# The 256-token level of a gated linear attention, taken through the state at token 256

## The chip, the cores and the metric

The kernel runs on one core of a Trainium2 chip. A core has TensorE (PE, matrix multiplication, results in PSUM), VectorE (DVE), ScalarE (ACT), GpSimd (POOL) and SyncE (SP, which here issues DMAs). The metric is the device time of one execution in microseconds (us), as the median of several runs.

## The reference

One decoder layer over 512 tokens of width 1024: a layer norm, then gated linear attention (GLA) and latent attention side by side, then an MLP. The change lies in the GLA, four heads with keys of 128 and values of 256:

```python
def step(state, inp):
    qi, ki, vi, gi = inp
    b = jnp.cumsum(gi, axis=2)
    b_last = b[:, :, -1:, :]
    diff = b[:, :, :, None, :] - b[:, :, None, :, :]
    decay = jnp.exp(jnp.where(causal[:, :, None], diff, -jnp.inf))
    scores = jnp.einsum('bhid,bhjd,bhijd->bhij', qi, ki, decay)
    o = jnp.einsum('bhij,bhjv->bhiv', scores, vi) + jnp.einsum('bhid,bhdv->bhiv', qi * jnp.exp(b), state)
    state = jnp.exp(b_last)[:, :, 0, :, None] * state + jnp.einsum('bhjd,bhjv->bhdv', ki * jnp.exp(b_last - b), vi)
    return state, o
```

In short, token i receives for each earlier token j the value v_j with the weight sum over d of q_id k_jd times the decay of channel d from j to i.

## The kernel before

Activations lie with features on the 128 partitions and the 512 tokens along the free dimension, in blocks of 128 tokens. Nearly every product is taken in three matmuls: each fp32 operand is split into a high part (a copy rounded to the format fp32r, on ACT) and a low part (the remainder, on DVE), by the helper `split` (lines 109 to 115), and high x high, high x low and low x high are summed in PSUM.

**Levels.** The kernel doesn't use chunks of 64 but a tree over the tokens. For s = 1, 2, 4 ... 256, level s covers the pairs (j in the left half, i in the right half) of each stretch of 2s tokens. `gla_levels(h)` (line 790) keeps one tile `qk` a head, [128, 2, 512]: plane 0 holds keys, plane 1 queries. `update(s)` multiplies left keys and right queries by their decays, so that before level s the keys carry the decay to the end of their half and the queries the decay from its start; a level is then a plain product of keys and queries. Levels up to 64 are put with masks into the four diagonal 128x128 blocks `SD`, later split to `sd`; level 128 makes the two blocks `s128`; level 256 makes the four blocks of scores between tokens 0 to 255 and tokens 256 to 511 in plain fp32 (lines 872 and 873: for each key block, 128 keys against 256 queries), and `take` splits them into `s256` (lines 829 and 830).

**Output.** `gla_out(h)` (line 896) sums the output of query block i over the key blocks j <= i: scores (weights) times values `vh`, `vl` (moving, 256 columns), three matmuls a block pair, ten block pairs a head. Two query blocks share a PSUM bank (`ps`). Then come the mean square (line 920), the gate, and transposes into `ogT` (line 936), which `y_gla` reads after the gates' projections and `mla_qr(0)`.

**What sets the order.** The levels and the outputs are two lanes of generators (`lane_levels`, `lane_out`, one head after the other) that are stepped from inside the projections' matmul loops, `gemm_tm` (lines 281 to 283), `proj_r` (752 to 754) and the gates' `unit` (1210 to 1212). The order so traced gives priorities; the order on each engine is then fixed at build by a scheduler that follows a simulated timeline (line 1681). PSUM tiles come from two pools of four banks, `MM` for projections and `PX` for nearly all of the GLA. Weights are loaded into three `wraw` buffers and split on ACT and DVE at lines 191 and 192, ahead of their use.

Of the kernel before, what the change touches and what calls it, by code (L numbers as in the profile page):

```python
# [52 lines left out]
def tile_hybrid_block(ctx: ExitStack, tc: tile.TileContext, I, out, dbg=None):  # L53
# [19 lines left out]
    def A(shape, dt=F32, n="a"):  # L73
        tag, bufs = ("C", 8) if n in TAG_C else (n, TAG_W[n]) if n in TAG_W else ("A", 24)
        return pa.tile(shape, dt, tag=tag, bufs=bufs, name=nm(n))
# [14 lines left out]
    def PX(shape=(P, T), dt=F32, n="px"):  # L90
        return px.tile(list(shape), dt, tag="px", name=nm(n))
# [17 lines left out]
    def split(src, hi, lo, scale=None):  # L109
        if scale is None:  # L110
            act(hi, src, AF.Copy)
            return vtt(lo, src, f(hi), op=ALU.subtract)
        else:
            act(hi, src, AF.Copy, scale=scale)
            return stt(lo, src, scale, f(hi), op0=ALU.mult, op1=ALU.subtract)
# [674 lines left out]
    def gla_levels(h):  # L790
        qk = QK[h]
        QK[h] = None
        if h == 0:
            decays(0)
        D, DS[h] = DS[h], None
        k0 = qk[:, 0, :]
        off = {s: 2 * T - 2 * T // s for s in (1, 2, 4, 8, 16, 32, 64, 128)}
        SD = B([P, NT, P], F32, "SD")
        s128 = s256 = None

        def update(s):
            v = lr(qk, s)
            vtt(v, v, view(D, off[s] + 1, (2, T // (2 * s)), (-1, 2), (0, s)), op=ALU.mult)

        def pack(s):
            M = B([P, T], F32, "M")
            if s == 128:
                act(M.rearrange("p (n two s) -> p n two s", two=2, s=s), lr(qk, s), AF.Copy)
            else:
                for i, w in enumerate((T + 256 + s, T + s - 256)):  # L810
                    act(pairs(M[:, i * 256:(i + 1) * 256], s), view(k0, i * 256, (2 * s, 128 // s), (w, 2), (1, s)), AF.Copy)
            return M

        def put(dst, src, s, w):
            mk = (lmask, lmask2)[1 - w][:, LEVELS.index(s), :].rearrange("p (n s) -> p n s", s=s)
            nc.vector.copy_predicated(dst.rearrange("p t (n two s) -> p t n two s", two=2, s=s)[:, :, :, w, :],
                                      mk[:, None].to_broadcast([P, 2, 64 // s, s]), src)

        def take(s, p):
            nonlocal s128, s256  # L820
            if s <= 64:
                v = p[:, :256].rearrange("p (t n two s) -> p t n two s", t=2, two=2, s=s)
                for i, w in enumerate((1, 0)):
                    put(SD[:, 2 * i:2 * i + 2], v[:, :, :, w, :], s, w)
            elif s == 128:
                s128 = B([P, 2, 2, P], F32R, "s128")
                split(p[:, :256].rearrange("p (a b) -> p a b", b=P), s128[:, 0], s128[:, 1])
            else:
                s256 = A([P, 2, 2, 2 * P], F32R, "s256")
                split(p.rearrange("p (a b) -> p a b", b=256), s256[:, 0], s256[:, 1])  # L830

        x0 = B([P, T], F32, "x0")
        act(x0.rearrange("p (a c) -> p a c", a=2), view(k0, 0, (T + 256, 2), (1, 256)), AF.Copy)
        xs = [B([P, 2, 192], F32, "x1") for _ in range(2)]
        for i, x in enumerate(xs):
            c = 2 * i * P
            act(x[:, :, :P], qk[:, 1 - i, c:c + 256].rearrange("p (t i) -> p t i", i=P), AF.Copy)
            vtt(x[:, :, P:], view(qk[:, 1 - i, :], c + 1 - i, (P, 2), (2, 64)), view(D, c + 1, (P, 2), (2, 64)), op=ALU.mult)
        v = view(k0, 0, (2, T // 2), (T, 2))
        vtt(v, v, view(D, 1, (2, T // 2), (-1, 2)), op=ALU.mult)  # L840
        v = view(k0, T + 1, (2, T // 2))
        vtt(v, v, D[:, T:T + T // 2], op=ALU.mult)
        Ms = [pack(2)]
        yield
        px1 = []
        for i in range(2):
            p = PX()
            for t in range(2):
                c = (2 * i + t) * P
                mm(p[:, t * 192:(t + 1) * 192], x0[:, c:c + P], xs[i][:, t, :], start=True, stop=True)  # L850
            px1.append(p)
        update(2)
        Ms.append(pack(4))
        yield
        for i, p in enumerate(px1):
            pt = p[:, :384].rearrange("p (t c) -> p t c", c=192)
            d = SD[:, 2 * i:2 * i + 2, :]
            vtt(d, pt[:, :, :P], ident[:, None, :].to_broadcast([P, 2, P]), op=ALU.mult)
            put(d, pt[:, :, P:].rearrange("p t (n s) -> p t n s", s=1), 1, 1 - i)
        prev, s = None, 2  # L860
        while s < T:
            p = PX()
            M = Ms.pop(0) if s < 256 else None
            if s <= 64:
                for i in range(2):
                    mm(p[:, i * P:(i + 1) * P], M[:, i * P:(i + 1) * P], M[:, 256 + i * P:256 + (i + 1) * P], start=True, stop=True)
            elif s == 128:
                for i in range(2):
                    mm(p[:, i * P:(i + 1) * P], M[:, 2 * i * P:(2 * i + 1) * P],
                       M[:, (2 * i + 1) * P:(2 * i + 2) * P], start=True, stop=True)  # L870
            else:
                for j in range(2):
                    mm(p[:, j * 256:(j + 1) * 256], qk[:, 0, j * P:(j + 1) * P], qk[:, 1, 256:], start=True, stop=True)
            if s <= 64:
                update(2 * s)
            if s <= 32:
                Ms.append(pack(4 * s))
            if prev is not None:
                take(*prev)
            prev = (s, p)  # L880
            s *= 2
            if s == 16 and h + 1 < GH:
                decays(h + 1)
            yield
        sd = A([P, 2, NT, P], F32R, "sd")
        act(sd[:, 0, :2], SD[:, :2], AF.Copy)
        gtt(sd[:, 1, :2], SD[:, :2], f(sd[:, 0, :2]), op=ALU.subtract)
        take(*prev)
        p = PX()
        for i in range(2):  # L890
            nc.tensor.transpose(p[:, i * P:(i + 1) * P], SD[:, 2 + i, :], ident)
        yield
        split(p[:, :256].rearrange("p (t i) -> p t i", i=P), sd[:, 0, 2:], sd[:, 1, 2:])
        SS[h] = (sd, s128, s256)

    def gla_out(h):
        while SS[h] is None or Vh[h] is None or rgn[h] < NT:
            yield
        sd, s128, s256 = SS[h]

        def blk(j, i, w):
            if i == j:
                return sd[:, w, i, :]
            if j // 2 == i // 2:
                return s128[:, w, j // 2, :]
            return s256[:, w, j, (i - 2) * P:(i - 1) * P]

        vh, vl = Vh[h]
        ss = S([P, NT], F32, "gss")
        ps = []  # L910
        for i in range(NT):
            if i % 2 == 0:
                ps.append(PX())
            o = ps[i // 2][:, (i % 2) * HV:(i % 2 + 1) * HV]
            for j in range(i + 1):
                mm(o, blk(j, i, 0), vh[:, j, :], start=j == 0, stop=False)
                mm(o, blk(j, i, 0), vl[:, j, :], start=False, stop=False)
                mm(o, blk(j, i, 1), vh[:, j, :], start=False, stop=j == i)
            sq = B([P, HV], F32, "osq")
            act(sq, o, AF.Square, accum_out=ss[:, i:i + 1])  # L920
            if i >= 1:
                yield
        vts(ss, ss, 4.0 / HV, 4.0 * RMS_EPS, op0=ALU.mult, op1=ALU.add)
        rs = S([P, NT], F32, "grs")
        gtt(rs, ss, mhalf[:, :NT], op=ALU.pow)
        yield
        og = [B([P, 2, HV], F32, "og") for _ in range(2)]
        for i in range(NT):
            o = ps[i // 2][:, (i % 2) * HV:(i % 2 + 1) * HV]
            stt(og[i // 2][:, i % 2, :], o, rs[:, i:i + 1], Rg[h][:, i, :], op0=ALU.mult, op1=ALU.mult)  # L930
        yield
        for kk in range(2):
            k = 2 * h + kk
            p = PX()
            for tt in range(NT):
                nc.tensor.transpose(p[:, tt * P:(tt + 1) * P], og[tt // 2][:, tt % 2, kk * P:(kk + 1) * P], ident)
            yield
            o = A([P, 2, T], F32R, "ogT")
            split(p, o[:, 0, :], o[:, 1, :], scale=glg[:, k:k + 1])
            ogT[k] = o  # L940
# [744 lines left out]
```

## Time and profile before

| | |
|---|---|
| median of 3 runs | 876.1 us (875.27 to 876.38) |
| the profiled execution | 876.66 us, of which the span 874.4 us |
| granted TensorE clock | 0.998 |
| TensorE busy | 857.4 us (98%) |
| DVE busy | 633.8 us (72%) |
| ACT busy | 469.4 us (54%) |
| line 873, matmuls of level 256 | 16 records, 120.5 to 206.2 us |
| lines 916 to 918, output blocks | 40 records each, 172.9 to 242.8 us |

A time in the trace counts from the start of the span. In a timeline's rows come start, duration, engine, line, operation, output and inputs by the program's names, shape and count; in brackets idle time of the engine before it and what ended it. Names lose their numbers, so `s` stands for `s128` and `s256`, and `px` for any tile of that pool. A matmul with fp32 operands appears as two records. Durations of matmuls overlap, so what one adds is read from the distance of the starts, or from the chain of waits, which counts each stretch of time once. Rows of waits give engine, tile and line, what was waited for, the total in us, the times and the longest.

### The profile page before, as it was taken

Reading aid. Unit: us, or ns where it says so; the run is one execution under the profiler, and the core shown is the slowest. Engines: PE = TensorE matmul, PEld = TensorE weight load, DVE = VectorE, ACT = ScalarE, POOL = GpSimd, SP = SyncE. Lnnn points to the kernel's source line nnn. Section 1 sums busy time; section 2 is a strip of 40 time slices with the busy share of each in tenths; the row PEclk is TensorE's granted clock in tenths of the full one; section 3 lists DMA queues with packets and bytes.
Section 4 is the critical chain, followed back from the end, with each engine's and each line's share of the span. In section 5 each row is a group of like instructions: output and inputs, shape, how many; then the busy total and the mean of one; then the engine's idle time right before and its main releaser. Section 6 shows DMA issues by size and latency. Waiting matters only on the chain.

```text
span 874.4 us, 12828 instructions
## 1 busy us (share of the span) xinstructions
PE 857.4 (98%) x4765; PEld 748.0 (86%) x4765; DVE 633.8 (72%) x1037; ACT 469.4 (54%) x821; POOL 143.8 (16%) x184
## 2 busy tenths in 40 slices
PE   6999999999999999999999999999999999999996
PEld 5988888889999988888888889988888888889985
DVE  7859989968566547567667878986567546788865
ACT  6546767746565625346545324575366446666820
POOL 0323304210110030300000022005301520141000
PEclk9999999999999999999999999999999999999999
DMA  7994946696646444323126446008922990498311
GB/s 248 273 240 143 335 149 157 202 276 209 145 146 151 135 112 126 80 55 103 49 85 256 142 143 219 1 1 243 262 73 49 296 212 22 101 240 223 118 62 76
DMA packets 95213, 134.57 MB, mean 154 GB/s; under 512 B 12672, under 2 KB 58112, under 8 KB 95152
## 3 DMA queue, kind: packets, MB, share of 16 engines
q1 hardware_dynamic: 73840, 92.36, 33.3%
q0 software_dynamic: 19392, 37.76, 19.9%
q10 hardware_dynamic: 1920, 3.66, 1.1%
q8 instruction: 37, 0.61, 0.3%
q14 instruction: 24, 0.20, 0.1%
HBM read 110.15 MB, written 8.91 MB: 136 GB/s over the span
## 4 chain that ended last, share of the span: by engine, by line
PE 91%; DVE 4%; DMA 3%; issue 1%; ACT 1%; SPq 0%; POOLq 0%; DVEq 0%; POOL 0%; ACTq 0%
PE mm L247 11%; PE mm L248 11%; PE mm L249 11%; PE mm L283 5%; PE mm L281 5%; PE mm L282 5%; PE mm L1212 4%; PE mm L1210 4%; PE mm L1211 4%; PE px L1496 2%; PE px L1497 2%; PE px L1498 2%; PE mm L754 1%; PE mm L753 1%; PE mm L752 1%; DMA res<-ev 1%
## 5 line engine op out<-in xcount | busy, mean ns | idle before, releaser
L192 DVE TENSOR_TENSOR wlo<-wraw,whi 128x1024 fp32r<-128x1024 f32 (+1 forms) x90 | 98.7, 1098 | 92.5 <-ACT whi L191 86.0
L191 ACT ACTIVATE whi<-wraw 128x1024 fp32r<-128x1024 f32 (+1 forms) x90 | 85.4, 949 | 92.2 <-PE mm L248 43.2
L248 PE MATMUL mm<-h,whi 128*128 128x512 f32 x224 | 87.2, 389 | 0.0
L247 PE MATMUL mm<-h,whi 128*128 128x512 f32 x224 | 87.1, 390 | 0.0
L249 PE MATMUL mm<-h,wlo 128*128 128x512 f32 x224 | 83.2, 390 | 0.0
L192 DVE TENSOR_TENSOR wlo<-wq,whi 128x1024 fp32r<-128x1024 f32 x44 | 54.0, 1227 | 28.9 <-ACT whi L191 28.8
L1515 POOL DMA_DIRECT2D res<-ev x42 | 37.5, 1030 | 184.8 <-ACT ev L1513 153.8
L191 ACT ACTIVATE whi<-wq 128x1024 fp32r<-128x1024 f32 x44 | 46.5, 1056 | 27.8 <-PE mm L1211 15.9
L1212 PE MATMUL mm<-sh,wlo 128*128 128x256 f32 x176 | 50.0, 284 | 0.0
L1211 PE MATMUL mm<-sh,whi 128*128 128x256 f32 x176 | 49.8, 283 | 0.0
L1210 PE MATMUL mm<-sh,whi 128*128 128x256 f32 x176 | 49.8, 283 | 0.0
L249 PEld LDWEIGHTS mm<-h,wlo 128*128 128x128 f32 x224 | 42.0, 188 | 9.1 <-DVE wlo L192 0.4
L248 PEld LDWEIGHTS mm<-h,whi 128*128 128x128 f32 x224 | 42.1, 188 | 8.7
L247 PEld LDWEIGHTS mm<-h,whi 128*128 128x128 f32 x224 | 42.0, 188 | 8.6
L191 ACT ACTIVATE xh<-wraw 128x1024 fp32r<-128x1024 f32 (+1 forms) x28 | 27.4, 986 | 28.2 <-PE mm L283 15.7
L192 DVE TENSOR_TENSOR xl<-wraw,xh 128x1024 fp32r<-128x1024 f32 (+1 forms) x28 | 31.3, 1128 | 8.7 <-ACT xh L191 8.7
L1558 ACT ACTIVATE relu<-mm 128x512 f32<-128x512 f32 x24 | 14.1, 595 | 41.9 <-PE mm L249 41.9
L1210 PEld LDWEIGHTS mm<-sh,whi 128*128 128x128 f32 x176 | 33.8, 192 | 0.0
L1211 PEld LDWEIGHTS mm<-sh,whi 128*128 128x128 f32 x176 | 33.8, 192 | 0.0
L1212 PEld LDWEIGHTS mm<-sh,wlo 128*128 128x128 f32 x176 | 33.8, 192 | 0.0
L1212 PE MATMUL mm<-h,wlo 128*128 128x256 f32 x112 | 31.8, 284 | 0.0
L1210 PE MATMUL mm<-h,whi 128*128 128x256 f32 x112 | 31.8, 284 | 0.0
(481 smaller groups left out, 2699.0 us busy)
## 6 DMA issues: line engine op xcount, KB each, us to landing
wraw<-in_w_ff_dram SPq DMA_DIRECT2D x36, 512.0 KB, 4.9
wraw<-in_w_in_dram SPq DMA_DIRECT2D x30, 512.0 KB, 5.5
wq<-in_w_ff_dram POOLq DMA_DIRECT2D x26, 512.0 KB, 9.0
res<-ev POOLq DMA_DIRECT2D x42, 256.0 KB, 10.0
wq<-in_w_in_dram SPq DMA_DIRECT2D x20, 512.0 KB, 7.1
wq<-in_w_in_dram POOLq DMA_DIRECT2D x18, 512.0 KB, 9.8
hsd<-hs SPq DMA_DIRECT2D x16, 256.0 KB, 4.0
xr<-hsd SPq DMA_DIRECT2D x16, 256.0 KB, 4.9
```

The source lines that it names most:

```text
L191: st["ins"] = act(hi[:, :nk, :n], raw[:, :nk, :n], AF.Copy)
L192: st["lo"] = vtt(lo[:, :nk, :n], raw[:, :nk, :n], f(hi[:, :nk, :n]), op=ALU.subtract)
L247: mm(o, hi[:, c], xh, start=first, stop=False)
L248: mm(o, hi[:, c], xl, start=False, stop=False)
L249: mm(o, lo[:, c], xh, start=False, stop=last)
L281: mm(o, xh, hi[:, :n], start=opens, stop=False, skip_group_check=share)
L282: mm(o, xh, lo[:, :n], start=False, stop=False, skip_group_check=share)
L283: mm(o, xl, hi[:, :n], start=False, stop=last, skip_group_check=share)
L1210: mm(oa, hi[:, k, c], xh, start=opens and k == 0 and a == 0, stop=False, skip_group_check=True)
L1211: mm(oa, hi[:, k, c], xl, start=False, stop=False, skip_group_check=True)
L1212: mm(oa, lo[:, k, c], xh, start=False, stop=k == 3, skip_group_check=True)
L1515: nc.gpsimd.dma_start(res[tt + t][:, j * T:(j + 1) * T], e, accum_op=ALU.add)
```

## The change

Level 256 makes no scores. The two blocks of scaled keys are transposed on TensorE (lines 872 and 873), so that tokens lie on the partitions; `take` splits the transposed keys into `s256[:, 0]` and the scaled queries of tokens 256 to 511 into `s256[:, 1]`. `gla_out` first sums keys times values over the two blocks into a new `PX` tile `p`: the state at token 256, 128x256. It is split into `sh` and `sl`, which take the place of the transposed keys in `s256`. Query blocks 2 and 3 then get one term, scaled queries times state, in place of two blocks of scores times values; `terms(i)` lists the terms of block i in their new order.

```diff
@@ take
-                s256 = A([P, 2, 2, 2 * P], F32R, "s256")
-                split(p.rearrange("p (a b) -> p a b", b=256), s256[:, 0], s256[:, 1])
+                s256 = A([P, 2, 2, 256], F32R, "s256")
+                split(qk[:, 1, 256:], s256[:, 1, 0], s256[:, 1, 1])
+                split(p[:, :256], s256[:, 0, 0], s256[:, 0, 1])
@@ gla_levels
                 for j in range(2):
-                    mm(p[:, j * 256:(j + 1) * 256], qk[:, 0, j * P:(j + 1) * P], qk[:, 1, 256:], start=True, stop=True)
+                    nc.tensor.transpose(p[:, j * P:(j + 1) * P], qk[:, 0, j * P:(j + 1) * P], ident)
@@ gla_out
-        def blk(j, i, w):
-            if i == j:
-                return sd[:, w, i, :]
-            if j // 2 == i // 2:
-                return s128[:, w, j // 2, :]
-            return s256[:, w, j, (i - 2) * P:(i - 1) * P]
-
         vh, vl = Vh[h]
+        p = PX()[:, :HV]
+        for j in range(2):
+            kh, kl = [s256[:, 0, w, j * P:(j + 1) * P] for w in range(2)]
+            mm(p, kh, vh[:, j, :], start=j == 0, stop=False)
+            mm(p, kh, vl[:, j, :], start=False, stop=False)
+            mm(p, kl, vh[:, j, :], start=False, stop=j == 1)
+        sh, sl = s256[:, 0, 0], s256[:, 0, 1]
+        split(p, sh, sl)
+
+        def terms(i):
+            if i % 2:
+                yield (s128[:, 0, i // 2], s128[:, 1, i // 2]), (vh[:, i - 1, :], vl[:, i - 1, :])
+            yield (sd[:, 0, i], sd[:, 1, i]), (vh[:, i, :], vl[:, i, :])
+            if i >= 2:
+                c = slice((i - 2) * P, (i - 1) * P)
+                yield (s256[:, 1, 0, c], s256[:, 1, 1, c]), (sh, sl)
+
         ss = S([P, NT], F32, "gss")
         ps = []
         for i in range(NT):
             if i % 2 == 0:
                 ps.append(PX())
             o = ps[i // 2][:, (i % 2) * HV:(i % 2 + 1) * HV]
-            for j in range(i + 1):
-                mm(o, blk(j, i, 0), vh[:, j, :], start=j == 0, stop=False)
-                mm(o, blk(j, i, 0), vl[:, j, :], start=False, stop=False)
-                mm(o, blk(j, i, 1), vh[:, j, :], start=False, stop=j == i)
+            ts = list(terms(i))
+            for n, ((ah, al), (wh, wl)) in enumerate(ts):
+                mm(o, ah, wh, start=n == 0, stop=False)
+                mm(o, ah, wl, start=False, stop=False)
+                mm(o, al, wh, start=False, stop=n == len(ts) - 1)
```

## The prediction, made before any run of the change

> **What bounds the kernel now.** I read the page first, then the waits of TensorE, then its busy time by stage, and last the order of its instructions where the edited code runs.
>
> ```profile
> span 874.4 us, 12828 instructions
> PE 857.4 (98%) x4765; PEld 748.0 (86%) x4765; DVE 633.8 (72%) x1037; ACT 469.4 (54%) x821; POOL 143.8 (16%) x184
> PE 91%; DVE 4%; DMA 3%; issue 1%; ACT 1%; SPq 0%; POOLq 0%; DVEq 0%; POOL 0%; ACTq 0%
> ```
>
> TensorE is busy for 857.4 of 874.4 us and makes up 91% of the chain that ended last. A matmul's busy time overlaps its neighbour's, so this alone doesn't say that it never starves; its waits do:
>
> ```profile
> PE px L446 <- ACT x L435: 8.4, 1, 8.4
> PE px L1212 <- DVE wlo L192: 0.7, 1, 0.7
> PE px L446 <- DVE lnt L453: 0.3, 1, 0.3
> PE mm L247 <- ACT h L449: 0.3, 1, 0.3
> PE mm L247 <- DVE rt L976: 0.2, 1, 0.2
> ```
>
> That is the whole list. After the 8.4 us at the start nothing in the kernel holds TensorE for more than 0.7 us, and no row names a line of the GLA code. By stage (columns: TensorE, weight load, DVE, ACT, POOL, each with its count, then granted clock, DMA share, GB/s):
>
> ```profile
> 120.00:140.00 20.00, 20.00 (x101) 17.00 (x100) 19.73 (x37) 16.09 (x34) 7.16 (x9) 1.00 0.63 187
> 160.00:180.00 20.00, 20.00 (x109) 17.16 (x108) 17.41 (x37) 12.54 (x26) 3.36 (x3) 1.00 0.90 242
> 240.00:260.00 20.00, 20.00 (x169) 20.00 (x169) 13.23 (x19) 13.65 (x25) 3.36 (x3) 1.00 0.41 130
> ```
>
> The edited lines run from 120.7 to 250 us (first and last row of the next fence). TensorE is full there at the full clock (1.00); DVE comes second, 19.73 of 20 us at 120 to 140. So a microsecond of TensorE work taken out here is a microsecond of time, as long as what it waits for keeps up.
>
> **What is removed and added on TensorE.** The chain view charges each instruction only the time that it adds:
>
> ```profile
> 120.68 0.86 PE px L873 x4
> 144.74 0.86 PE px L873 x4
> 170.89 0.86 PE px L873 x4
> 205.75 0.86 PE px L873 x4
> 249.11 0.87 PE px L936 x8
> ```
>
> Line 873 issues two matmuls a head, which the trace records as four; they take 0.86 us a head. In their place come two 128x128 transposes against `ident`, the same form as those of line 936, of which eight took 0.87 us, or 0.109 each: 0.22 a head. Removed: 0.86 - 0.22 = 0.64 us a head, 2.56 us for four.
>
> The Trainium skill speaks against that price: "TensorE: Matmul & The Clock Gate", Part 4 (PE-mode transpose), gives about 275 ns for a transpose inside a kernel and says that transposes don't count as activity for the clock gate. By its figure the eight transposes would take 2.2 us and the estimate of the saving would be 3.44 - 2.2 = 1.2 us; the granted clock of 1.00 at 240 to 260, with the run of eight in it, doesn't show the second half of the rule.
>
> In `gla_out` the number of matmuls stays. Before: ten blocks by three, 30 a head. After: two blocks of keys times values (6), then 1 + 2 + 2 + 3 blocks of output (24), again 30. All have 128x128 weights and 256 columns, as these have:
>
> ```profile
> 206.81 0.28 PE L916 MATMUL px<-vh,s 128*128 128x256 f32 x1
> 206.93 0.28 PE L917 MATMUL px<-vl,s 128*128 128x256 f32 x1
> ```
>
> One starts every 0.12 us, whatever it multiplies, so an equal count costs nothing.
>
> **What is added on ACT and DVE.** Before, the level's product is split by one pass of 512 columns on each engine. After, there are three passes of 256: the scaled queries, the transposed keys, the state.
>
> ```profile
> 170.01 0.39 ACT L111 ACTIVATE s<-px 128x256 fp32r<-128x256 f32 x1
> 171.79 0.60 ACT L111 ACTIVATE s<-px 128x512 fp32r<-128x512 f32 x1 [0.27 <-PE px L873]
> 172.75 0.38 PE L891 MATMUL px<-ca,SD 128*128 128x128 f32 x2
> 173.03 0.41 DVE L112 TENSOR_TENSOR s<-px,s 128x256 fp32r<-128x256 f32 x1
> 173.93 0.37 ACT L111 ACTIVATE sd<-px 128x256 fp32r<-128x256 f32 x1
> 174.03 0.68 DVE L112 TENSOR_TENSOR s<-px,s 128x512 fp32r<-128x512 f32 x1
> 176.42 0.41 DVE L112 TENSOR_TENSOR sd<-px,sd 128x256 fp32r<-128x256 f32 x1
> ```
>
> ACT: 3 x 0.39 - 0.60 = 0.57 us more a head, with the pass that reads `qk` in SBUF taken at the PSUM price. DVE: 3 x 0.41 - 0.68 = 0.55 us more a head, 2.2 us in all. Neither sets the end here, so I take both at nothing; what hides them is that weights are split ahead of their use. The two closest places that I found:
>
> ```profile
> 184.52 1.06 ACT L191 ACTIVATE whi<-wraw 128x1024 fp32r<-128x1024 f32 x1 [3.62 <-DMA wraw<-in_w_in_dram]
> 185.61 1.23 DVE L192 TENSOR_TENSOR wlo<-wraw,whi 128x1024 fp32r<-128x1024 f32 x1 [3.52 <-ACT whi L191]
> 188.67 0.39 PE L282 MATMUL mm<-wlo,h 128*128 128x512 f32 x1
> ...
> 204.46 1.22 DVE L192 TENSOR_TENSOR wlo<-wraw,whi 128x1024 fp32r<-128x1024 f32 x1
> 208.13 0.28 PE L1212 MATMUL mm<-h,wlo 128*128 128x256 f32 x1
> ```
>
> From the end of the low half to its first use: 1.83 and 2.44 us. TensorE's lead there would be 1.92 and 2.56 us (0.64 for each head whose level is past). So even if those splits didn't move forward at all, each would be missed by only 0.1 us; and the transfer that the first waits for is itself issued when a buffer comes free, which moves with TensorE. If the cover were gone, the price would be the 2.2 us of DVE.
>
> **The new wait.** The state has to leave PSUM, be split on ACT and then DVE, and come back as an operand. TensorE works in its program's order, so when it reaches the state's first use too early, every projection matmul queued behind stands with it, and with these the ACT and DVE passes that empty their banks. Emission puts twelve of the head's own matmuls between (three for block 0, six for block 1, three for the diagonal of block 2): 12 x 0.12 = 1.44 us of cover. How long is the chain? In the rows above, the product of line 873 ends at 171.75 (170.89 + 0.86 in the chain) and its split at 174.71: 2.96 us. The transposes of line 891 end at 173.13 and their split at 176.83: 3.70 us. The short case is
>
> ```profile
> 118.02 0.60 PE L869 MATMUL px<-M 128*128 128x128 f32 x4
> 119.08 0.42 DVE L112 TENSOR_TENSOR s<-px,s 128x256 fp32r<-128x256 f32 x1 [0.21 <-ACT s L111]
> ```
>
> 118.62 to 119.50, 0.88 us. So the wait is bounded by 0 (0.88 is under 1.44) and, by the row that the state's form is nearest to, 2.96 - 1.44 = 1.5 us a head. Which end? The order isn't that of emission: it is fixed at build along a simulated timeline (line 1681), and the trace shows that a head's blocks are taken apart by projection work:
>
> ```profile
> 173.32 0.40 PE L282 MATMUL mm<-wlo,h 128*128 128x512 f32 x1
> ...
> 175.63 0.28 PE L916 MATMUL px<-vh,s 128*128 128x256 f32 x1
> 175.87 0.40 PE L281 MATMUL mm<-whi,h 128*128 128x512 f32 x1
> ```
>
> Block 0 of the first head ends where the projection takes over at 173.32, and the head's next block starts 2.3 us later, behind ten projection matmuls of 0.23 us. The old level had the same kind of chain (product, ACT, DVE, operand), four times, and no row of TensorE's waits names its use. I take 0.05 us a head, 0.2 in all, nearest to that empty list.
>
> **Banks and buffers.** The state takes one more of the four `PX` banks until its low half is made; with the level lane's two and the output lane's two that would be five where both lanes run (the last head's line 873 at 205.75 stands beside output blocks at 206.81), so one lane starts later and projection work goes ahead. I take that at nothing: the last head's transposes end at 250.0 (249.11 + 0.87), and their result is read by `y_gla`, traced only after the last gates and `mla_qr(0)`. `qk` is held until its split, at most the 3 us of the chain above. No DMA is added or moved.
>
> **Sum.** The profiled run took 876.66 us: a span of 874.4 and 2.3 around it. 876.66 - 2.56 + 0.2 = 874.3. The median of the runs, 876.1, lies 0.56 below the profiled one, so the forecast is **873.7 us**; its own range, with waits of 0 to 0.8 us in all and up to half a microsecond of better order, is 873.0 to 874.3.
>
> **Rivals.**
>
> *The splits become the bound.* If DVE, at 19.73 of 20 us, stays where it is and does 2.2 us more ahead of the weights that TensorE needs, the lead is lost: 2.2 us by the extra passes, so 876.1 - 2.56 + 2.2 = 875.7; with half of them in the way, 874.6. I set it at **875.2**. For it: the windows at 120 to 140 us. Against: the slacks of 1.83 and 2.44 us, almost the whole lead, and DVE's idle 2.6 us at 160 to 180 (17.41 of 20).
>
> *TensorE waits for the state*, the slower side. One mechanism: a head's state use comes straight behind its twelve own matmuls while DVE is full. Price 1.5 us a head by the chain of 2.96: 4 x 1.5 - 2.56 = 3.4 us slower, **879.6**. It decides from 0.64 us a head, a chain of 1.44 + 0.64 = 2.08 us without foreign matmuls in between. For it: two of the three chains above are longer than that. Against: the ten projection matmuls between two blocks, and the empty list.
>
> *The transposes don't do what they should.* If a transpose cost its whole duration instead of its spacing,
>
> ```profile
> L891 PE MATMUL px<-ca,SD x8: 270/271/272, 122.8 to 211.2; 128*128 128x128 f32 x8
> ```
>
> eight would take 8 x 0.27 = 2.16 us and the saving be 3.44 - 2.16 = 1.28: **874.8**. Against it stands the run of eight in 0.87 us. The Trainium skill's page on TensorE, named above, is on its side.
>
> **How the numbers follow.** The runs spread over 1.1 us, so 0.2% (1.75 us: 874.35 and 877.85) is about what a measurement can tell from no change. Chances: the forecast 0.62; the splits 0.16; the state's wait 0.17; the transposes 0.05. The forecast lies under 874.35, so faster has 0.62. The splits (874.6 to 875.7) and the transposes lie within 0.2%: 0.21. The state's wait is slower at four heads and within the bound if it bites at two or three, by which I move 0.02 of it: same 0.23, slower 0.15. The range goes from 872.4 (the forecast's own lower end less half of the runs' spread) up to 877.6, between the state's wait at two heads (2 x 1.5 - 2.56: 876.5) and at three (878.0); what is left out is most of that rival and a little at the lower end.
>
> **What would show it.** In the chain of the changed kernel the four pieces of 0.86 us for the level are gone, and pieces of two transposes, 0.22 us, stand there. Matmuls of the first `gla_out` loop, six a head, follow at 0.12 us. The list of TensorE's waits gets no row of more than 0.3 us for the output lines; a row there that names DVE's or ACT's split of the state, 0.6 us or more a head, proves the slower rival. A row that names line 192 in the window 160 to 215 proves the splits. The span should read 872.0. Wrong in another way would be a difference that lies behind 255 us, where nothing is edited: then the new order, not the work, has moved the time.

## The result and the profile after

The changed kernel takes 882.69 us (median of four runs, 881.44 to 884.05) against 875.84: a ratio of 1.0079, 95% interval 1.0061 to 1.0096. The forecast was 873.7 with a range up to 877.6; the change is slower, not faster. The profiled execution took 881.44 us, its span 879.6, that is 5.2 more than before. (The medians differ by 6.9: the profiled execution of the kernel before, 876.66, lies above its four other runs, and that of the changed kernel is the fastest of its four. The account below is of the 5.2.)

The page of the changed kernel, its span and busy times:

```profile
span 879.6 us, 12827 instructions
PE 857.2 (97%) x4757; PEld 747.1 (85%) x4757; DVE 632.8 (72%) x1045; ACT 470.1 (53%) x829; POOL 144.8 (16%) x184
```

No engine is busy for over 1.0 us more than before (ACT 0.7 more, POOL 1.0 more, DVE 1.0 less), yet the span is 5.2 longer, so TensorE must stand still or run slowly somewhere. TensorE's waits (us in total, times, longest):

```profile
PE mm L281 <- ACT whi L191: 2.7, 1, 2.7
PE mm L1224 <- DVE wlo L192: 1.3, 2, 0.8
PE px L928 <- ACT osq L932: 1.1, 1, 1.1
PE mm L1222 <- ACT whi L191: 0.8, 2, 0.5
```

Behind the start (8.4 us as before) stand four new rows with 5.9 us together, where the kernel before had none over 0.7. (Lines behind 870 are shifted: 916 to 918 are now 928 to 930, 920 is 932, 1210 to 1212 are 1222 to 1224.) By stage, with the columns of the prediction's table:

```profile
160.00:180.00 20.00, 17.64 (x96) 14.93 (x94) 12.02 (x31) 9.38 (x20) 6.41 (x5) 1.00 1.03 282
180.00:200.00 20.00, 19.57 (x92) 16.39 (x93) 14.67 (x27) 11.68 (x28) 1.04 (x1) 0.91 0.80 193
200.00:220.00 20.00, 18.82 (x144) 17.83 (x144) 15.87 (x37) 11.86 (x30) 1.75 (x2) 1.00 0.67 217
240.00:260.00 20.00, 17.89 (x143) 17.10 (x143) 11.52 (x18) 12.36 (x27) 1.04 (x1) 1.00 0.12 28
```

TensorE is idle for 2.36 + 0.43, 1.18 and 2.11 us in three places, and in the second row its clock is 0.91. DVE and ACT are far from full there.

**First place, 177.6 to 185.4.** SyncE's queue, first of the kernel before and then of the changed one. `wraw` are the projection's weights, `wq` those of the gates, each issue 512 KB:

```profile
162.58 0.38 SPq L176 DMA_DIRECT2D wraw<-in_w_in_dram  x1
163.01 1.01 SPq L1183 DMA_DIRECT2D wq<-in_w_in_dram  x2
164.96 0.37 SPq L176 DMA_DIRECT2D wraw<-in_w_in_dram  x1
165.38 4.17 SPq L1183 DMA_DIRECT2D wq<-in_w_in_dram  x4
```

```profile
160.19 0.38 SPq L176 DMA_DIRECT2D wraw<-in_w_in_dram  x1
160.66 4.97 SPq L1195 DMA_DIRECT2D wq<-in_w_in_dram  x6
165.78 3.13 SPq L176 DMA_DIRECT2D wraw<-in_w_in_dram  x3
```

The diff touches no transfer, but the rebuilt order puts the second pair of projection weights behind six transfers instead of two. TensorE reaches the place about 2.5 us earlier (line 873 of the third head started at 170.89; its transposes start at 168.32), and the pair is issued 0.8 us later. ACT and TensorE of the changed kernel, from their timelines:

```profile
173.25 0.38 ACT L932 ACTIVATE osq<-px 128x256 f32<-128x256 f32 x1 [2.04 <-PE px L930]
...
179.27 1.06 ACT L191 ACTIVATE whi<-wraw 128x1024 fp32r<-128x1024 f32 x1 [5.54 <-DMA wraw<-in_w_in_dram]
...
183.13 0.37 ACT L932 ACTIVATE osq<-px 128x256 f32<-128x256 f32 x1
...
187.23 0.37 ACT L932 ACTIVATE osq<-px 128x256 f32<-128x256 f32 x1
```

```profile
177.36 0.28 PE L930 MATMUL px<-vh,sd 128*128 128x256 f32 x1
180.38 1.21 PE L281 MATMUL mm<-whi,h 128*128 128x512 f32 x4 [2.74 <-ACT whi L191]
181.64 0.56 PE L282 MATMUL mm<-wlo,h 128*128 128x512 f32 x1
182.00 0.63 PE L283 MATMUL mm<-whi,h 128*128 128x512 f32 x1
182.42 0.63 PE L282 MATMUL mm<-wlo,h 128*128 128x512 f32 x1
```

ACT stands 5.54 us at the split, waiting for the transfer, and TensorE 2.74 us for ACT. Then the matmuls start every 0.43 us where 0.23 is usual, up to 185.39: nine steps from 181.64 in 3.75 us instead of 2.07, 1.7 us lost. The granted clock says why:

```profile
182.00:184.00 2.00, 2.00 (x6) 1.62 (x5) 0.74 (x1) 1.83 (x4) 0.00 (x0) 0.50 1.19 241
```

Notice also the three rows of line 932, the mean squares of the first head's output blocks 0, 1 and 2: blocks 1 and 2 were done on TensorE by 177.64, but their mean squares stand behind the late split in ACT's order. (The rows don't number the blocks; the last of the three, at 187.23, is taken for block 2's by the order of the program.) It matters later.

**Second place, 205.3 to 206.7.** After the projection's last matmul the second head's output runs with no projection work between its first blocks:

```profile
205.31 0.28 PE L930 MATMUL px<-vh,sd 128*128 128x256 f32 x1
206.65 0.39 PE L928 MATMUL px<-vh,s 128*128 128x256 f32 x1 [1.06 <-ACT osq L932]
```

Block 0 is done; block 1's first matmul waits for ACT to have read block 0, which lies in the other half of the same PSUM bank. **Third place, 245 to 256:** four waits of 0.31, 0.76, 0.47 and 0.57 us for weight splits of the gates.

The sum: -2.56 from the prediction's sum, + 2.74 + 0.34 (from 181.3, a wait for the split's low half) + 1.7 at the first place, + 1.06 at the second and a wait of 0.28 for the state's low half at 208.4, + 2.11 at the third: 5.7 us, where the span is 5.2 longer. Behind 260 us no stall was added.

### The profile page after: what moved, and what is told of

Its sections match the earlier page's. It is cut to its first block, busy times and chain, and to the rows that moved or that the text cites. A ratio compares the mean times of both kernels' runs of the same rounds, so it can differ in the third digit from the quotient of the medians.

```text
span 879.6 us, 12827 instructions
## 1 busy us (share of the span) xinstructions
PE 857.2 (97%) x4757; PEld 747.1 (85%) x4757; DVE 632.8 (72%) x1045; ACT 470.1 (53%) x829; POOL 144.8 (16%) x184
## 4 chain that ended last, share of the span: by engine, by line
PE 93%; DVE 3%; DMA 2%; ACT 1%; issue 1%; SPq 0%; POOLq 0%; POOL 0%; DVEq 0%; ACTq 0%
PE mm L247 11%; PE mm L248 11%; PE mm L249 11%; PE mm L283 5%; PE mm L282 5%; PE mm L281 5%; PE mm L1224 4%; PE mm L1223 4%; PE mm L1222 4%; PE px L1508 2%; PE px L1509 2%; PE px L1510 2%; DMA wraw<-in_w_in_dram 2%; PE mm L1508 2%; PE mm L1509 2%; PE mm L1510 2%
```

## The experiments

The kernel before ran again on the same chip beside each group; its medians there were 875.5 to 875.7 us.

**1. Is it the order of the transfers?** My first theory: yes, at the first place. The rival: the state's wait or the added splits. One run puts the old order back, one gives the kernel before the new order.

The changed kernel, with the six transfers (`u_load`) issued after the second pair, except those that were ahead of it before:

```diff
-    u_load("g0", "22")
-    u_load("g0", "t3")
+    with tc.issue_after(stream[PL["v", 1]["idx"][1]]["dma"].ins):
+        u_load("g0", "22")
+        u_load("g0", "t3")
```

> The changed kernel with one edge more: the four last of the six transfers into wq for the first gate ("22" and "t3") are issued on SP behind the transfer of the second weight pair of the second values projection, as they stood in the kernel before. Theory A (the loss comes from that pair being issued behind six transfers instead of two): the 2.7 us wait of L281 for whi and the half clock after it are gone; the time falls by at least 4.4 us, to 878 or less, and down to 873.5 if the later waits at 205 to 210 and 244 to 256 us went with it. Theory B (the wait for the state, or the fifth PX bank, costs the time, and the transfer order is a bystander): 881 to 883 as before the edge.

Measured: 878.93 us, ratio 1.0038 (1.0023 to 1.0053). 3.76 us of the loss are gone, less than the 4.4 or more that I expected. Its stages:

```profile
180.00:200.00 20.00, 19.52 (x103) 16.45 (x103) 15.99 (x30) 11.04 (x25) 3.62 (x3) 1.00 0.92 261
200.00:220.00 20.00, 18.74 (x157) 18.33 (x156) 15.32 (x35) 12.80 (x34) 2.35 (x3) 1.00 0.66 211
240.00:260.00 20.00, 17.89 (x144) 17.11 (x143) 12.10 (x17) 12.61 (x25) 1.52 (x2) 1.00 0.28 88
```

The first place is full to 0.5 us at the full clock; the second and third are as they were.

The kernel before, with its second pair held back until six `wq` transfers have been issued:

```diff
-        while st["dma"] < min(len(stream), n):
+        while st["dma"] < min(len(stream), n, st["hold"]):
...
+    st["hold"] = 10 ** 6
+    with tc.issue_after(st["u"].ins):
+        fetch(PL["v", 1]["idx"][1] + 1)
```

> The kernel before, with only the order of transfers on SP changed: the second weight pair of the second values projection is issued behind all six transfers into wq. Theory A: TensorE waits 2 to 3 us for whi at about 180 us, its clock drops afterwards, and the time rises by 4 to 7 us, to 880 to 883. Theory B: within 1 us of the kernel before, 875 to 877.

Measured: 879.28 us, ratio 1.0043 (1.0028 to 1.0058), 3.8 us slower without any change of the level, a little less than expected. Its one new wait and its clock:

```profile
PE mm L281 <- ACT whi L191: 2.0, 1, 2.0
```

```profile
184.00:186.00 2.00, 2.00 (x6) 1.52 (x6) 2.00 (x4) 1.25 (x3) 0.00 (x0) 0.50 1.22 220
```

So the order costs this much in either kernel as it stands. In this one, too, the head's last output block (twelve matmuls here) runs only at 189.66, behind a mean square at 186.08 on ACT. Some 3.4 us over the kernel before are left in the run with the order put back, 6.0 with the 2.56 of work saved. TensorE is idle for 1.26 and 2.11 us at the other two places and for 0.48 at the first; the rest isn't located.

**2. Which half of the change brings them?** The level alone: the kernel before with the transposes and their splits, and the old output loop, which reads them where the scores stood (so the scores of level 256 are left out):

```diff
-                    mm(p[:, j * 256:(j + 1) * 256], qk[:, 0, j * P:(j + 1) * P], qk[:, 1, 256:], start=True, stop=True)
+                    nc.tensor.transpose(p[:, j * P:(j + 1) * P], qk[:, 0, j * P:(j + 1) * P], ident)
...
-            return s256[:, w, j, (i - 2) * P:(i - 1) * P]
+            return s256[:, j, w, (i - 2) * P:(i - 1) * P]
```

> Only the level's half of the change: two transposes and three splits of 256 columns; the output keeps its ten blocks of scores times values, reading the transposed keys and the queries where the scores of level 256 were (these scores are left out). No state, no new wait, no fifth bank. The order of transfers on SP comes out as in the changed kernel, six in front. Theory A: slow like the changed kernel, 879 to 883, with the wait of L281 for whi. Theory B: the saving of 2.6 us without the loss, 873 to 874.5.

Measured: 883.01 us, ratio 1.0081 (1.0064 to 1.0098). The state alone: the changed kernel with the level's fp32 product in place of the transposes:

```diff
-                    nc.tensor.transpose(p[:, j * P:(j + 1) * P], qk[:, 0, j * P:(j + 1) * P], ident)
+                    mm(p[:, j * 256:(j + 1) * 256], qk[:, 0, j * P:(j + 1) * P], qk[:, 1, 256:], start=True, stop=True)
```

> Only the output's half of the change: the state, its split and the new terms, with level 256 still as two fp32 products of 256 columns, whose first half stands where the transposed keys would (the transposition is left out). TensorE has as much to do as in the kernel before. On SP the second weight pair is issued ahead of all six transfers into wq. Theory A: no wait for whi near 180 us, 875 to 878. Theory B: the state's wait and the fifth bank are all here, so 880 or more.

Measured: 880.32 us, ratio 1.0057 (1.0042 to 1.0072). Two stages of each, the level alone first:

```profile
200.00:220.00 20.00, 18.95 (x140) 17.60 (x140) 18.02 (x41) 12.83 (x32) 1.75 (x2) 1.00 0.70 220
240.00:260.00 20.00, 17.89 (x144) 17.11 (x143) 13.23 (x19) 12.98 (x28) 1.04 (x1) 1.00 0.12 38
```

```profile
200.00:220.00 20.00, 19.17 (x150) 18.15 (x149) 15.69 (x36) 13.02 (x33) 1.75 (x2) 1.00 0.66 211
240.00:260.00 20.00, 17.90 (x144) 17.12 (x143) 12.13 (x17) 11.60 (x26) 1.03 (x1) 1.00 0.24 69
```

Both places starve in both. The state isn't their cause, since the first kernel has none; nor are the transposes, since the second has none. By its number the second run fell to theory B, by its waits it didn't: no row names the state's split. The third place shows the same waits of 0.8 and 1.3 us for splits of the gates' weights as in the changed kernel; at the second place the rows are these:

```profile
PE px L928 <- DVE SD L816: 0.6, 1, 0.6
PE px L928 <- ACT osq L932: 0.2, 1, 0.2
```

These waits come to 2.9 us of the 4.8; the rest isn't located. What the two kernels share is the new splits in `take` and a program laid out anew. A new layout alone needn't starve the two places: the kernel before with its transfers swapped is one, and TensorE is busy for 20.00 of 20 us there at 200 to 220 and at 240 to 260.

**3. Can the third place be mended by order?** In the changed kernel a split of the gates' weights stands on ACT ahead of a copy (`u2`) that frees TensorE's next products; before, it stood behind. To the kernel with the transfers put back, one edge is added that holds the split back:

```diff
+                if key == "g0" and op == "t3" and g == 1:
+                    st["gates"] = (u2["ins"],)
```

> The kernel with the transfers' order put back, and in it one more edge: the split of the weights that the gates of the next unit need stands on ACT behind the copy of u2's second half, as in the kernel before. If the three stretches are independent (my theory), the window 240 to 260 gets back about 2 us of TensorE (20.0 for 17.9) and the time falls from 878.9 by 2.1 to about 876.8, with the 1.2 us around 205 to 209 still there. Rival, that ACT's and DVE's added passes have no room and a stall only moves: the window fills, but another wait of 1 to 2 us appears behind 210 us and the time stays at 878 to 879.

Measured: 877.45 us, ratio 1.0022 (1.0013 to 1.0031), 1.5 us better instead of 2.1. The waits for the gates' splits are gone, and the third place is still short: 18.22 of 20 us. Its TensorE and ACT there:

```profile
241.13 0.28 PE L930 MATMUL px<-vh,sd 128*128 128x256 f32 x1
243.19 0.39 PE L928 MATMUL px<-vh,s 128*128 128x256 f32 x1 [1.78 <-ACT osq L932]
```

```profile
241.50 0.38 ACT L932 ACTIVATE osq<-px 128x256 f32<-128x256 f32 x1 [3.08 <-PE px L930]
...
241.88 0.89 ACT L1264 ACTIVATE gt<-e,hbg 128x256 f32<-128x256 f32 x2
242.67 0.37 ACT L932 ACTIVATE osq<-px 128x256 f32<-128x256 f32 x1
```

The same wait as at the second place: a block's first matmul waits until ACT has read its neighbour in the bank, and on ACT a tanh of the gates is ahead of that read. Most of the stall had only changed its name, as the rival said, though the time lies nearer to my theory's 876.8 than to the rival's 878 to 879.

The state summed and split earlier, ahead of the previous head's mean square, on top of that:

```diff
+        state(h + 1)
         vts(ss, ss, 4.0 / HV, 4.0 * RMS_EPS, op0=ALU.mult, op1=ALU.add)
```

> As the run before, and the state of a head is summed and split as soon as its operands are there, ahead of the previous head's mean square. If the stall around 205 to 209 comes from where the state's products and its split stand behind the output of the head before, the row of line 928 or 929 of some 1.0 us leaves TensorE's waits and the time is about 875.6 (876.8 less 1.2), the same as before within 0.2%; if the whole saving of 2.56 us then comes through, 873.5 to 874. Rival, the stall is the projection's end, where nothing is left to fill TensorE whatever the order: a wait of about 1 us stays between 204 and 212 us and the time stays at 876.5 to 877.5.

Measured: 879.22 us, ratio 1.0040 (1.0027 to 1.0054): slower than either side had said. The waits for mean squares fell from 2.8 to 0.2 us and 240 to 260 us is full, but waits for other lines' splits took their place (1.4 us of line 281, 0.9 us of line 752 and smaller ones). Moving work by hand moved the stalls.

**4. The bank as the cause.** New theory: a head's output blocks share banks in pairs, so the second of a pair can't start before ACT has read the first, and ACT's queue, whatever it waits for, becomes TensorE's. The next kernels take that away by issuing the two mean squares of a bank together, behind its second block:

```diff
-            sq = B([P, HV], F32, "osq")
-            act(sq, o, AF.Square, accum_out=ss[:, i:i + 1])
+            if i % 2:
+                for b in range(2):
+                    sq = B([P, HV], F32, "osq")
+                    act(sq, ps[i // 2][:, b * HV:(b + 1) * HV], AF.Square, accum_out=ss[:, i - 1 + b:i + b])
```

With both orders put back:

> The kernel with both orders put back (transfers, gates), and the mean squares of two output blocks that share a PSUM bank issued together after the second block, so that a block's first matmul doesn't wait for ACT to have read its neighbour. Theory: both stalls that are left, 1.0 us at 203 and 1.8 us at 243, are that wait; with it gone the rows of line 928 waiting for ACT's osq leave the list, and the time falls by 2.8 from 877.45 to about 874.6; if TensorE is then as full as in the kernel before, the whole saving of 2.56 comes through: 872.9. Rival, ACT has too much to do there and the wait only changes its name: 876.5 to 877.5.

Measured: 874.41 us, ratio 0.9984 (0.9976 to 0.9993). The control, the same edit in the kernel before:

> The kernel before with the mean squares paired in the same way and nothing else: the control. TensorE's list of waits before had no row of the output lines, so there is nothing to gain: 875.5, the same within 0.2%. If it is faster by more, then what the run beside it gains is not the level's but the pairing's; if slower, the build's new order costs here too without any change of the level.

Measured: 876.09 us, ratio 1.0011 (0.9998 to 1.0024). And without the edge for the gates:

> The kernel with the transfers' order put back and the mean squares paired, without the edge for the gates. If the split of the gates' weights stands ahead of the u2 copy only because of where the output blocks waited, the stall of 2.1 us at 245 to 256 goes with the pairing alone: about 874.6, as the run with both. If it has a cause of its own, it stays: about 876.7.

Measured: 874.17 us, ratio 0.9981 (0.9973 to 0.9990). Its two longest waits behind the start and two stages:

```profile
PE px L1226 <- DVE wlo L192: 0.6, 1, 0.6
PE mm L282 <- DVE wlo L192: 0.5, 1, 0.5
```

```profile
200.00:220.00 20.00, 20.00 (x161) 19.47 (x160) 15.00 (x30) 14.02 (x35) 1.75 (x2) 1.00 0.56 177
240.00:260.00 20.00, 20.00 (x170) 20.00 (x169) 13.59 (x17) 12.66 (x20) 3.04 (x3) 1.00 0.46 144
```

Second and third place are full. The pairing alone gains nothing in the kernel before, so what is gained here is taken to be the level's saving, no longer given back. The edge for the gates wasn't needed.

Then the pairing as the only edit of the changed kernel, its transfers left in the late order:

> The changed kernel with the mean squares paired and nothing else: the transfers stand as in the changed kernel, the second weight pair behind six others. If the late transfer and the stalls behind 200 us are independent, this is the kernel without them (874.2) plus the 3.8 us that the order of the transfers cost in two runs so far: 878.0, with one wait of 2 to 3 us of line 281 for ACT's whi at about 180 us and no row of the output lines. Rival, the pairing moved TensorE's work so that the late pair is missed by less: 875 to 876.

Measured: 874.15 us, ratio 0.9985 (0.9975 to 0.9996). Here I was wrong by 3.8 us: the pair is as late as ever (issued at 166.07, split from 180.56) and costs almost nothing. TensorE there, and the stretches before and behind:

```profile
178.69 1.47 PE L851 MATMUL px<-x,x 128*128 128x192 f32 x8
181.67 1.20 PE L281 MATMUL mm<-whi,h 128*128 128x512 f32 x4 [1.52 <-ACT whi L191]
```

```profile
178.00:180.00 2.00, 2.00 (x16) 1.86 (x14) 0.48 (x1) 0.00 (x0) 1.28 (x1) 1.00 1.14 276
...
182.00:184.00 2.00, 1.94 (x9) 1.27 (x8) 0.88 (x1) 0.58 (x1) 0.00 (x0) 1.00 1.19 245
```

At 178 to 180, where the changed kernel had no matmul at all, TensorE is full, up to 178.69 with block 3 of this head's output and then with line 851, the first products of a later head's levels. In the changed kernel the three terms of block 3, nine matmuls, couldn't run there: they had to wait for block 2's mean square, at 187.23 on ACT, behind the splits that waited for the transfer, and they ran at 191.05. Line 851 ran at 189.06 there: ACT made its operands only behind the late split (184.01, here 176.04), so that over half of the filling is owed to ACT's new order and not directly to the bank. Nine matmuls take 1.1 us and line 851 some 1.5; the split starts 1.3 us later than in the changed kernel; so the gap is 1.52 us instead of 2.74, and in this execution the clock doesn't fall.

**5. The same by another way.** The pairing gives a new layout too, so the time could be luck. Blocks laid crosswise, 0 and 2 in one bank, 1 and 3 in the other; the mean squares stay as they were:

```diff
-            if i % 2 == 0:
+            if i < 2:
                 ps.append(PX())
-            o = ps[i // 2][:, (i % 2) * HV:(i % 2 + 1) * HV]
+            o = ps[i % 2][:, (i // 2) * HV:(i // 2 + 1) * HV]
```

> The changed kernel with the output blocks laid crosswise into their two PSUM banks (0 and 2 in one, 1 and 3 in the other) and nothing else; the mean squares stay one by one. No block then follows directly on a block of its own bank. If the stalls come from a block's first matmul waiting for ACT's read of the block just before it in the same bank, they go here as with the paired squares: 874 to 875.5, no row of line 928 waiting for osq, and at most 2 us of line 281 waiting for the late weight pair at about 180 us. Rival, the pairing helped by the order that its build happened to give: this build has another order, and the time lies anywhere between 876 and 883, with stalls behind 200 us again.

Measured: 875.64 us, ratio 0.9997 (0.9987 to 1.0007), 7 us below the changed kernel. Its only new wait, a slice behind it, and two stages:

```profile
PE mm L281 <- ACT whi L191: 1.8, 1, 1.8
```

```profile
184.00:186.00 2.00, 2.00 (x6) 1.61 (x6) 2.00 (x4) 1.14 (x5) 0.00 (x0) 0.57 1.21 208
```

```profile
200.00:220.00 20.00, 20.00 (x155) 19.25 (x154) 16.12 (x31) 12.72 (x32) 1.75 (x2) 1.00 0.59 187
...
240.00:260.00 20.00, 20.00 (x169) 20.00 (x169) 13.69 (x19) 13.67 (x25) 2.35 (x2) 1.00 0.35 107
```

Both later places are full again, and block 3 runs ahead of the gap (177.80 to 179.04, line 851 behind it at 181.92); the late pair is left, with a gap of 1.85 us and the lower clock. The crossing was not tried in the kernel before. With the transfers' order put back as well:

> The changed kernel with the output blocks crosswise in their banks and the transfers' order put back. The run with crossed banks alone had one wait left, 1.85 us for the late weight pair, and behind it some 4 us at about half the clock (about 1.5 us lost). If the late pair is all that is left, both go and a rest of 0.5 us may stay: 875.6 - 1.85 - 1.5 + 0.5 = 872.8, near 875.5 - 2.56 = 872.9, the whole saving of TensorE's work. Rival, the room is used up and another wait takes its place, as in the kernel with paired squares, where the same order made no difference (874.17 and 874.15): 874 to 875.5.

Measured: 874.23 us, ratio 0.9985 (0.9976 to 0.9994): 1.4 us better where I expected 2.8, and inside the rival's range. No wait behind the start is longer than 0.5 us, and TensorE is idle for 0.64 us at 180 to 200.

## Why the prediction was wrong

**The term that held.** The level costs what was worked out. Line 874 in the changed kernel:

```profile
168.32 0.38 PE L874 MATMUL px<-ca,qk 128*128 128x128 f32 x2
168.46 0.48 PE L752 MATMUL mm<-whi,h 128*128 128x512 f32 x1
168.77 0.39 PE L753 MATMUL mm<-wlo,h 128*128 128x512 f32 x1
```

From 168.32 to 168.77 pass 0.45 us, of which the projection's matmul takes 0.23: two transposes, 0.22, as forecast. So the rival of slow transposes is out. The page of the profile agrees: TensorE is busy for 857.4 us before and for 854.4 to 855.3 in the four fastest kernels (the three paired ones, and the crossed one with its transfers put back). Their spans, 872.1 to 872.4, lie near the 872.0 that I named, but partly by luck: that was taken from a profiled span of 874.4, while the median span of the kernel before in the runs beside them is 873.7 to 873.9.

**The step that failed** is the sentence "No DMA is added or moved", with the one by which a transfer of the same queue "moves with TensorE". It holds for the diff, not for the built program. I had written myself that the order is fixed at build along a simulated timeline, and used this for the matmuls between two blocks, but costed every queue as if it kept its order. The second weight pair went from behind two to behind six transfers of 512 KB, while TensorE came 2.5 us earlier: 3.8 us by experiment 1, as long as the output blocks share banks in the old way, and nothing in the paired kernels (874.17 and 874.15).

**"Banks and buffers ... at nothing"** was the deeper miss. I counted the banks, and not who waits for whom inside one. The waits for a neighbour's mean square (1.06 us at the second place, 1.78 in the kernel of experiment 3) and the nine matmuls stuck at the first are one mechanism; two edits that touch only the output's mean squares or its banks remove it and bring the changed kernel from 882.69 to 874.15 and 875.64. All six kernels with the change, or half of it, and the old sharing take 877.45 to 883.01; all five with the change and one of the two edits take 874.15 to 875.64. The Trainium skill has the rule, in "PSUM — Partial Sum Buffer", section "PSUM bank collisions raise a hardware error": accesses of two engines are to be kept apart by bank, not by address. The traces agree: the matmul that waits 1.06 us at 206.65 writes other columns than those that ACT reads.

**That "weights are split ahead of their use"** failed at the third place: there TensorE waits 2.11 us for splits of the gates' weights, and no wait for a mean square stands among the four. The passes themselves were priced too high: 2.3 us more of ACT and 2.2 of DVE in the prediction, 0.7 more and 1.0 less busy time on the page.

**The rivals.** The state's wait was the slower rival, and it isn't what happened: the one wait for it is 0.28 us at 208.4, near the 0.2 in the sum, and the level alone, without a state, takes 883.01. The splits as a bound (875.2) neither: DVE has 4.1 to 8.5 of 20 us free in the four stages shown first. My mark for it, a row that names line 192, would have misled: such rows appear (1.3 us), but outside the window that I gave, and for weights of the gates, whose splits ACT began only when TensorE's line 1223 had ended (2.18 us idle before the one at 244.10). And "wrong in another way" was sought behind 255 us; the new order did its harm between 177 and 256. (The price of the slower rival, 3.4 us on 876.1, gives 879.5 and not 879.6; nothing hangs on it.)

**What stays open.** Why the bank wait bites at the second place in the new layouts and not in the old, which shares its banks in the same way, wasn't isolated; the level alone has 1.0 us of it, the state alone 0.2. That the third place fills in all five kernels with either edit is shown; by what chain a bank shared by output blocks makes the gates' splits late there isn't. And in the medians the best kernels gain 1.3 to 1.5 us of the 2.56; TensorE's idle 0.6 to 1.6 us at 180 to 200 us in them, where the kernel before has none, bring the sums to 2.2 to 2.9.

## What to carry to other kernels

Where a build lays out the instruction order anew, a small edit can move transfers and splits that it doesn't touch: price the place where a queue's order could flip, above all where the DMA engines are full (1.03 at 160 to 180 here), and compare the queues before looking for the cause in the edited lines. Don't let one engine's short read stand between two matmul groups: groups that follow each other belong in different banks, or the reads go behind the second. The changed kernel with paired mean squares is faster than both kernels compared here, than the kernel before by only 0.15%: 874.15 us.

## What the runs showed of the hardware

The clock can fall after a gap of 1.85 us. TensorE's idle time near 180 us and the granted clock behind it, one profiled execution each: 0.48 and 1.52 us, it stays at 1.00; 1.85, 2.05, 2.74 and 3.42 us, it falls to 0.50 (the 0.57 shown for the gap of 1.85 us is a slice in which the low clock ends). The low clock begins 2.0 to 4.3 us after the gap's start, when TensorE may be at work again, and lasts 3.4 us, after the longest gap 6.8. In the changed kernel this cost 1.7 us, over half as much as the gap itself. The Trainium skill, "TensorE: Matmul & The Clock Gate", section "HAM oscillation", warns of gaps over about 3.4 us; here a gap of 1.85 us was enough.

The gap's length may not be all that decides. In the clock records of these traces the falls near 180 us come 170.67 us after the clock's first rise in three kernels and 167.25 us after it in the fourth: 50 and 49 times 3.413 us, the length of the low clock itself. So in these traces the clock changed on a grid of 3.41 us, and six executions can't tell how long a gap must be from where it must lie on that grid.
